# A hybrid decoder layer in fp32 on one core: the scheduler lays out the engines' streams by its timeline estimate instead of its plain one

## The chip, the cores and the metric

The kernel runs on one core of one Trainium2 chip. A core has TensorE (PE: matmuls, with its weight loads shown as PEld), VectorE (DVE), ScalarE (ACT), GpSimd (POOL) and SyncE (SP), each with an instruction stream of its own that it works off in order, and 16 DMA engines. The metric is device time in microseconds for one execution of the whole program; lower is better.

## The reference, cut to what matters

One layer, batch 1, 512 tokens, width 2048, everything in fp32. The layer's input is normalised and multiplied with one wide weight. Half of the mixing is done by 8 gated-DeltaNet heads, half by 8 latent-attention (MLA) heads. Then come an output projection with a residual, and a SwiGLU feed-forward network (FFN) of width 5632.

```
# gated DeltaNet, per head, in chunks (the kernel uses chunks of 128)
a_mat = where(strict, (k*beta) @ k.T * decay, 0)
sol   = triangular_solve(a_mat + I, [v*beta, k*beta*exp(gc)])
for each chunk:                       # one after the other
    v_new = u_c - w_c @ state
    o     = (q_c*exp(gc_c)) @ state + intra_c @ v_new
    state = state*exp(g_last) + k_dec.T @ v_new
# MLA, per head: softmax of (q_nope.k_nope + q_rope.k_rope), causal, times v
# FFN: (silu(h @ w_gate) * (h @ w_up)) @ w_down
```

## The kernel before, in words

The result has to be close to fp32, so each fp32 weight tile `raw` is split into a high part `whi` (cast on ACT, L137) and a rest `wlo` (subtraction on DVE, L138); activations are split likewise (`hh`, `hl`). A product of two split tiles is three matmuls into the same PSUM tile (`mm3`, L144 to L146). Weights are loaded by SP's queue; `raw` has two buffers, `whi` and `wlo` three each.

The program comes in four stages: the transposes and the norm of the input; the DeltaNet stage, which is what the change and the prediction speak of most; the MLA heads with the output projection; the FFN.

In the DeltaNet stage PE has two kinds of work. One is projections, `project(hp)` for head pairs 0 to 3, each with parts q, k, v and z, and then two `latent` projections for MLA. Each part takes two PSUM tiles `acc` (there are four), runs 96 mm3 matmuls into them and hands them to DVE: `u` (L440) is the read that frees an `acc` of parts q, k and v, and from it `y` is built (L441, L444 three times) and goes through ACT into `kq` or `vt`. `u` and `y` have one buffer each, `kq` two per head of a pair.

The other is `delta(h)`, one per head. Its first part squares and transposes k, multiplies `kq` with itself (the kk matmuls), makes `bm` (L500), `Y` (L513) and `dd` (L516, a reduction to the 16x16 diagonal blocks), sends `dd` to DRAM and back in another layout (`dr`, `rep`, two DMAs issued by ACT), and inverts the diagonal blocks by 30 short dependent DVE operations (`xt` L524 and `xs` L526), which give `R` (L527). Its second part, the chain, doubles the blocks in three levels (transposes of `R` at L555, two groups of small matmuls at L149, with DVE and ACT between them), and then goes through four chunks (`vn`, `st`). At its end ACT sums squares (L606), POOL takes a root (L169), DVE scales (`es`, L612), PE transposes (L617), and DVE writes `mixg` (L618). All of these matmuls use the PSUM tag `bank`, four tiles.

`project` and `latent` (the generator `fill`) and the two `delta` of a pair are generators; the strings ORDER and LAST say in which order their pieces are written into the program:

```
ORDER = "0ppp0p1ppp01p1"
LAST = "0ppp0p1ppp01ppp1"
```

What order the instructions then have on each engine is not written in the kernel: the tile scheduler of the context opened at L998 takes the program, its dependences and its buffers, and lays out one stream per engine, by priorities from the program's order and by an estimate of when each instruction could run. Names such as `acc_3005` below are a tile with the number of its allocation: `whi_3007`, `whi_3037`, `whi_3067` and `whi_3097` are the four weight tiles of pair 2's part z, whose PSUM tiles are `acc_3004` and `acc_3005`; `acc_2487` and `acc_2488` are those of its part k; head 2 has `R_1923`, head 3 `dd_2418` and `xt_2422`, head 6 `R_3943` and head 7 `R_4416`.

## Time and profile before

| | |
|---|---|
| median of 3 runs | 2429.13 us (2429.03 to 2430.13) |
| the profiled execution's own time | 2431.77 us |
| its span | 2430.0 us, mean granted TensorE clock 0.995 |
| PE busy | 2377.5 us (98%), 11142 matmuls |
| DVE busy | 1137.5 us (47%) |
| ACT busy | 706.8 us (29%) |
| POOL busy | 84.6 us (3%) |
| DMA | 225.74 MB, mean 93 GB/s |

The span is the time from the first to the last instruction on the core; the execution's own time has 1.77 us more around it. A row of a window table gives the busy time of each engine in that stretch, and how many of its instructions ran there. "PEclk" is the granted TensorE clock as a share of its full 2.4 GHz.

### The profile page before, as it was taken

To read this page: it belongs to the slowest core of one execution; us is meant where nothing else is said; L and a number is where in the kernel's file an instruction comes from. 1 tells how busy PE (TensorE), PEld (TensorE's weight loads), DVE (VectorE), ACT (ScalarE), POOL (GpSimd) and SP (SyncE) were. 2 spreads that over 40 slices of the span, in tenths; PEclk is the share of its full clock that TensorE was granted. 3 is DMA by queue.
4 is the path that set the end of the run, shared out by engine and by line. 5 is a ranking of instruction groups with operands and counts; after the bars stand their busy time and mean duration, and the time that the engine had idled before them with its cause. 6 is when DMAs were issued, how large, how long until landed. Compare 5 with 4: busy or idle time off the path is not lost.

```text
span 2430.0 us, 27609 instructions
## 1 busy us (share of the span) xinstructions
PE 2377.5 (98%) x11142; PEld 1954.5 (80%) x11142; DVE 1137.5 (47%) x1850; ACT 706.8 (29%) x1155; POOL 84.6 (3%) x89
## 2 busy tenths in 40 slices
PE   8999999999999999999999999999999999999998
PEld 6777878787787778888888888888888888888886
DVE  6556565655556555433434343433333343434345
ACT  5333333332333334322222212222222222222223
POOL 0010101110000000000000000000000000000000
PEclk9999999999999999999999999999999999999999
DMA  5322322222422222333333333232333333333333
GB/s 168 89 62 70 88 70 80 78 80 78 143 61 67 73 65 87 104 96 100 99 95 96 96 95 101 90 104 87 104 93 103 98 96 95 95 97 95 104 96 112
DMA packets 199807, 225.74 MB, mean 93 GB/s; under 512 B 17280, under 2 KB 161920, under 8 KB 199552
## 3 DMA queue, kind: packets, MB, share of 16 engines
q1 hardware_dynamic: 194752, 214.02, 29.4%
q10 hardware_dynamic: 4928, 9.97, 1.3%
q8 instruction: 87, 1.43, 0.3%
q14 instruction: 40, 0.33, 0.0%
HBM read 219.50 MB, written 4.46 MB: 92 GB/s over the span
## 4 chain that ended last, share of the span: by engine, by line
PE 87%; DVE 6%; DMA 3%; ACT 2%; issue 1%; POOL 1%; ACTq 0%; SPq 0%; POOLq 0%; DVEq 0%
PE acc L145 20%; PE acc L146 20%; PE acc L144 20%; PE bank L145 6%; PE bank L146 6%; PE bank L144 6%; PE bank L149 4%; DVE wlo L138 1%; PE score L149 1%; DMA rep<-dr 1%; DMA raw<-in_w_down 1%; PE op L149 1%; DVE y L444 1%; DMA raw<-in_w_in 1%; ACT whi L137 0%
## 5 line engine op out<-in xcount | busy, mean ns | idle before, releaser
L138 DVE TENSOR_TENSOR wlo<-raw,whi 128x1024 fp32r<-128x1024 f32 x386 | 469.0, 1216 | 705.7 <-ACT whi L137 701.0
L137 ACT CAST whi<-raw 128x1024 fp32r<-128x1024 f32 x386 | 403.6, 1046 | 1195.2 <-PE acc L145 650.0
L145 PE MATMUL acc<-fl,whi 128*128 128x512 f32 x1408 | 548.3, 389 | 0.0
L146 PE MATMUL acc<-fh,wlo 128*128 128x512 f32 x1408 | 548.2, 389 | 0.0
L144 PE MATMUL acc<-fh,whi 128*128 128x512 f32 x1408 | 548.1, 389 | 0.0
L145 PEld LDWEIGHTS acc<-fl,whi 128*128 128x128 f32 x1408 | 264.4, 188 | 54.8
L146 PEld LDWEIGHTS acc<-fh,wlo 128*128 128x128 f32 x1408 | 264.4, 188 | 54.8
L144 PEld LDWEIGHTS acc<-fh,whi 128*128 128x128 f32 x1408 | 264.3, 188 | 54.5
L145 PE MATMUL acc<-hl,whi 128*128 128x512 f32 (+1 forms) x656 | 264.4, 403 | 0.0
L144 PE MATMUL acc<-hh,whi 128*128 128x512 f32 (+1 forms) x656 | 262.1, 400 | 1.8 <-ACT whi L137 1.8
L146 PE MATMUL acc<-hh,wlo 128*128 128x512 f32 (+1 forms) x656 | 263.6, 402 | 0.0
L146 PE MATMUL bank<-whi,al 128*128 128x512 f32 x640 | 249.2, 389 | 0.0
L145 PE MATMUL bank<-wlo,ah 128*128 128x512 f32 x640 | 249.2, 389 | 0.0
L144 PE MATMUL bank<-whi,ah 128*128 128x512 f32 x640 | 249.2, 389 | 0.0
L924 DVE SCALAR_TENSOR_TENSOR x<-bank,rstd,x 128x512 f32<-128x512 f32 x160 | 119.8, 750 | 151.6 <-PE bank L146 151.6
L144 PEld LDWEIGHTS acc<-hh,whi 128*128 128x128 f32 (+1 forms) x656 | 124.3, 190 | 25.7 <-ACT whi L137 2.2
L145 PEld LDWEIGHTS acc<-hl,whi 128*128 128x128 f32 (+1 forms) x656 | 124.3, 190 | 24.5
L146 PEld LDWEIGHTS acc<-hh,wlo 128*128 128x128 f32 (+1 forms) x656 | 123.9, 189 | 23.5
L144 PEld LDWEIGHTS bank<-whi,ah 128*128 128x128 f32 x640 | 120.2, 188 | 24.9
L145 PEld LDWEIGHTS bank<-wlo,ah 128*128 128x128 f32 x640 | 120.2, 188 | 24.9
L146 PEld LDWEIGHTS bank<-whi,al 128*128 128x128 f32 x640 | 120.2, 188 | 24.9
L144 PE MATMUL acc<-whi,mgh 128*128 128x512 f32 x256 | 102.3, 400 | 2.8 <-ACT mgh L283 2.3
(284 smaller groups left out, 2228.1 us busy)
## 6 DMA issues: line engine op xcount, KB each, us to landing
raw<-in_w_gate SPq DMA_DIRECT2D x88, 512.0 KB, 3.6
raw<-in_w_up SPq DMA_DIRECT2D x88, 512.0 KB, 3.6
raw<-in_w_down SPq DMA_DIRECT2D x88, 512.0 KB, 3.8
raw<-in_w_in SPq DMA_DIRECT2D x80, 512.0 KB, 3.8
raw<-in_w_out SPq DMA_DIRECT2D x32, 512.0 KB, 4.0
rep<-dr ACTq DMA_DIRECT2D x8, 512.0 KB
x<-in_x ACTq DMA_DIRECT2D x4, 1024.0 KB, 7.8
raw<-in_w_ukv SPq DMA_DIRECT2D x32, 128.0 KB, 2.5
```

Of the source, the lines that this page charges most:

```text
L137: nc.scalar.copy(hi[:, :k * n], raw[:, :k * n])
L138: nc.vector.tensor_tensor(out=lo[:, :k * n], in0=raw[:, :k * n], in1=hi[:, :k * n].bitcast(F32), op=ALU.subtract)
L144: nc.tensor.matmul(ps, lhsT=lh, rhs=rh, start=start, stop=False)
L145: nc.tensor.matmul(ps, lhsT=lh, rhs=rl, start=False, stop=False)
L146: nc.tensor.matmul(ps, lhsT=ll, rhs=rh, start=False, stop=stop)
L149: nc.tensor.matmul(ps, lhsT=l, rhs=r, start=start, stop=stop)
L444: nc.vector.scalar_tensor_tensor(out=y, in0=u[:, j:j + S], scalar=vec[:, 0, j * 24 + ct:j * 24 + ct + 1], in1=y, op0=ALU.mult, op1=ALU.add)
L924: nc.vector.scalar_tensor_tensor(out=x2[:, t4, cs], in0=a, scalar=rstd[:, t4:t4 + 1], in1=x2[:, t4, cs], op0=ALU.mult, op1=ALU.add)
```

## The change

One argument of the tile context. The kernel's functions, buffers and operations stay as they are.

```diff
--- before.py
+++ after.py
@@ -995,7 +995,7 @@
     args.append(nc.dram_tensor("out_0", (S, D), F32, kind="ExternalOutput").ap())
-    with tile.TileContext(nc) as tc:
+    with tile.TileContext(nc, schedule_with_timeline_sim=True) as tc:
         layer_kernel(tc, *args)
```

The matmuls, the DVE operations and the DMA issues are the same in number; ACT has six more loads of a function table (L490 and the like), 18 for 12. What moves is the order on each engine. Three places follow.

The first is PE at the start of head 2's chain. Before, pieces of pair 2's part q (`acc_2124`) stand between its steps:

```order
L555 MATMUL bank_2186<-fst_68,R_1923 128x128 x4
L149 MATMUL bank_2187<-R_1923,bm_1904 128x64 x4
L144 MATMUL acc_2124<-hh_80,whi_2297 128x512
L145 MATMUL acc_2124<-hl_81,whi_2297 128x512
L146 MATMUL acc_2124<-hh_80,wlo_2298 128x512
...
L149 MATMUL bank_2198<-Y_1924,T_1922 128x64 x4
L146 MATMUL acc_2124<-hh_80,wlo_2298 128x512
L144 MATMUL acc_2124<-hh_80,whi_2297 128x512
L145 MATMUL acc_2124<-hl_81,whi_2297 128x512
L555 MATMUL bank_2204<-fst_68,R_1923 128x128 x4
```

After the change, the same steps:

```order
L146 MATMUL acc_3004<-hh_80,wlo_3068 128x512
L555 MATMUL bank_2186<-fst_68,R_1923 128x128 x4
L149 MATMUL bank_2187<-R_1923,bm_1904 128x64 x4
L149 MATMUL bank_2198<-Y_1924,T_1922 128x64 x4
L555 MATMUL bank_2204<-fst_68,R_1923 128x128 x4
L149 MATMUL bank_2205<-R_1923,bm_1904 128x64 x4
L149 MATMUL bank_2216<-Y_1924,T_1922 128x64 x4
L555 MATMUL bank_2222<-fst_68,R_1923 64x64 x4
```

and the end of that chain, up to the next projection matmul (`vn_2279` is the chain's last chunk, `kq_1113` belongs to head 3):

```order
L149 MATMUL bank_2247<-vn_2279,es_1903 128x128
L149 MATMUL bank_2403<-kq_1113 128x256 x2
L149 MATMUL bank_2409<-kq_1113 128x256 x2
L471 MATMUL bank_2470<-fst_68,vt_1873 128x128 x4
L471 MATMUL bank_2476<-fst_68,kq_1113 128x128 x4
L617 MATMUL bank_2689<-fst_68,es_1903 128x128 x4
L144 MATMUL acc_3005<-hh_80,whi_3007 128x512
```

The projections have moved ahead of the chain: when it begins, PE has done parts q, k and v of pair 2 and three of the four weight tiles of part z's first PSUM tile, and the 34 rows from L555 to L617 hold no projection matmul.

The second place is DVE around head 3's `dd`. Before, weight rests and the substitution follow it, and the read of pair 2's part k (`u_2618`) stands late in the substitution:

```order
L516 TENSOR_REDUCE dd_2418<-Y_2417 128x64
L138 TENSOR_TENSOR wlo_2581<-raw_2579,whi_2580 128x1024
L607 TENSOR_SCALAR ssq_2381<-ssq_2381 128x4
L138 TENSOR_TENSOR wlo_2631<-raw_2629,whi_2630 128x1024
L524 TENSOR_TENSOR xt_2422<-rep_2420,xs_2421 128x60
...
L524 TENSOR_TENSOR xt_2422<-rep_2420,xs_2421 128x16
L440 TENSOR_TENSOR u_2618<-acc_2488,rbc_71 128x512
```

After the change:

```order
L516 TENSOR_REDUCE dd_2418<-Y_2417 128x64
L441 TENSOR_SCALAR y_2610<-u_2609,vec_70 128x512
L618 SCALAR_TENSOR_TENSOR mixg_292<-bank_2689,vec_70,zt_2116 128x512
L444 SCALAR_TENSOR_TENSOR y_2610<-u_2609,vec_70,y_2610 128x512
L607 TENSOR_SCALAR ssq_2381<-ssq_2381 128x4
L444 SCALAR_TENSOR_TENSOR y_2610<-u_2609,vec_70,y_2610 128x512 x2
L440 TENSOR_TENSOR u_2618<-acc_2488,rbc_71 128x512
L441 TENSOR_SCALAR y_2619<-u_2618,vec_70 128x512
L524 TENSOR_TENSOR xt_2422<-rep_2420,xs_2421 128x60
...
L524 TENSOR_TENSOR xt_2422<-rep_2420,xs_2421 128x44
L138 TENSOR_TENSOR wlo_3098<-raw_3096,whi_3097 128x1024
```

The read that frees the PSUM tile of part k now stands right behind head 2's whole end and head 3's `dd`, and the rest of part z's last weight tile stands behind five of the `xt`.

The third place is PE at the end of the stage, heads 6 and 7. Before, pieces of the second latent projection (`acc_4896`, `acc_4897`) and of the output projection stand around head 7's last step:

```order
L146 MATMUL acc_4897<-hh_80,wlo_4900 128x512
L144 MATMUL acc_4896<-hh_80,whi_4929 128x512
...
L617 MATMUL bank_5018<-fst_68,es_4396 128x128 x4
L144 MATMUL acc_5130<-whi_5119,mgh_5055 128x512
```

After the change the last matmul of the latent projections stands ahead of head 6's chain:

```order
L146 MATMUL acc_4897<-hh_80,wlo_4990 128x512
L555 MATMUL bank_4204<-fst_68,R_3943 128x128 x4
...
L617 MATMUL bank_4720<-fst_68,es_3923 128x128 x4
L149 MATMUL bank_4636<-dg_4635,cst_67 128x128 x3
L555 MATMUL bank_4726<-fst_68,R_4416 128x128 x4
...
L617 MATMUL bank_5018<-fst_68,es_4396 128x128 x4
L149 MATMUL bank_5077<-cst_67,ssl_5066 128x128 x4
L144 MATMUL acc_5130<-whi_5119,mgh_5055 128x512
```

Both chains, 66 rows, stand between it and the next mm3 matmul, that of the output projection.

## Rows read from the trace of the kernel before

**Rows 1.** Windows by stage: each engine's busy time, then clock, DMA share, GB/s.

```profile
core 0: us, PE busy (x) PEld busy (x) DVE busy (x) ACT busy (x) POOL busy (x), PEclk, DMA share, GB/s
0.00:101.70 101.70, 90.03 (x410) 73.10 (x411) 61.81 (x95) 44.93 (x76) 2.58 (x13) 1.00 0.47 138
101.70:635.40 533.70, 511.84 (x2677) 417.30 (x2676) 319.14 (x758) 189.41 (x414) 60.66 (x58) 0.98 0.28 76
635.40:929.00 293.60, 286.40 (x1456) 231.03 (x1457) 173.85 (x347) 99.38 (x220) 18.16 (x13) 1.00 0.27 81
929.00:2350.00 1421.00, 1421.00 (x6306) 1178.04 (x6306) 536.34 (x583) 344.82 (x396) 1.01 (x1) 1.00 0.32 97
2350.00:2430.00 80.00, 68.26 (x297) 55.05 (x295) 46.39 (x68) 28.30 (x51) 2.18 (x4) 0.96 0.35 112
```

**Rows 2.** Windows around two long waits of PE and a short one.

```profile
143.00:147.20 4.20, 0.48 (x3) 0.09 (x2) 3.89 (x13) 1.05 (x1) 0.11 (x1) 0.96 0.47 135
147.20:153.00 5.80, 5.80 (x20) 5.12 (x21) 1.39 (x2) 0.59 (x1) 1.06 (x1) 0.50 0.38 114
570.00:576.00 6.00, 1.28 (x6) 0.77 (x6) 5.51 (x12) 2.19 (x3) 0.00 (x0) 0.80 0.31 87
576.00:582.00 6.00, 5.98 (x25) 4.88 (x26) 2.00 (x8) 0.00 (x0) 1.01 (x1) 0.63 0.32 87
630.00:636.00 6.00, 3.71 (x19) 2.71 (x17) 3.14 (x4) 2.85 (x5) 0.00 (x0) 1.00 0.55 149
```

**Rows 3.** PE in order of time: head 2's chain, then head 3's kk matmuls.

```profile
272.67 0.60 PE L555 MATMUL bank<-fst,R 128*128 128x128 f32 x4
...
277.45 0.60 PE L555 MATMUL bank<-fst,R 128*128 128x128 f32 x4
...
281.25 0.41 PE L555 MATMUL bank<-fst,R 64*64 64x64 f32 x4
...
292.71 0.48 PE L149 MATMUL bank<-vn,es 128*128 128x128 f32 x2
...
297.74 1.13 PE L149 MATMUL bank<-kq 128*128 128x256 f32 x4 [0.32 <-DVE es L612]
```

**Rows 4.** DVE in order of time, behind head 2's chain.

```profile
294.83 0.17 DVE L608 SCALAR_TENSOR_TENSOR sso<-sso,ssq 128x4 f32<-128x4 f32 x1
...
296.56 1.12 DVE L612 TENSOR_SCALAR es<-bank,f 128x128 f32<-128x128 f32 x4 [0.90 <-POOL f L169]
297.61 0.68 DVE L440 TENSOR_TENSOR u<-acc,rbc 128x512 f32<-128x512 f32 x1
...
299.26 1.22 DVE L138 TENSOR_TENSOR wlo<-raw,whi 128x1024 fp32r<-128x1024 f32 x1
...
307.53 1.04 DVE L516 TENSOR_REDUCE dd<-Y 128x64 f32<-128x512 f32 x1
...
319.37 0.26 DVE L524 TENSOR_TENSOR xt<-rep,xs 128x60 f32<-128x60 f32 x1 [5.67 <-DMA rep<-dr]
```

**Rows 5.** DVE in order of time: head 2's substitution, up to `R`.

```profile
257.65 0.26 DVE L524 TENSOR_TENSOR xt<-rep,xs 128x60 f32<-128x60 f32 x1 [4.46 <-DMA rep<-dr]
...
266.66 1.07 DVE L527 TENSOR_TENSOR R<-xs,cst 128x512 f32<-128x512 f32 x1
```

**Rows 6.** Groups by line, DVE: count, busy us, mean ns.

```profile
L444 DVE SCALAR_TENSOR_TENSOR y<-u,vec,y 128x512 f32<-128x512 f32 x72 | 54.0, 750 | 1.6
...
L440 DVE TENSOR_TENSOR u<-acc,rbc 128x512 f32<-128x512 f32 x24 | 16.5, 688 | 2.8 <-PE acc L146 1.9
L441 DVE TENSOR_SCALAR y<-u,vec 128x512 f32<-128x512 f32 x24 | 11.6, 482 | 0.6 <-ACT kq L452 0.5
...
L618 DVE SCALAR_TENSOR_TENSOR mixg<-bank,vec,zt 128x512 f32<-128x512 f32 x8 | 6.0, 745 | 2.1 <-PE bank L617 2.1
```

**Rows 7.** Waits of PE by line and releaser: us in total, times, longest.

```profile
PE bank L555 <- DVE R L527: 6.0, 4, 3.7
...
PE score L149 <- ACT knh L283: 2.7, 4, 0.7
...
PE bank L145 <- DVE fl L138: 1.7, 2, 1.1
```

## The prediction

> **What bounds the kernel now.** I read the windows by stage first. From 929 to 2350 us, the FFN and the end of the output projection, PE is busy for all of the 1421 us, 6306 matmuls at 0.2253 us each [rows 1]. No order of the same matmuls can shorten that stretch; it can only stay or get longer. What an order can change lies in the DeltaNet stage (101.7 to 635.4), where PE is busy 511.84 of 533.70 us and so idle 21.9, in the MLA stage with 7.2 idle, and in the end with 11.7 [rows 1]. The clock of the DeltaNet stage is 0.98, so some 10 us of it went to half speed (0.02 of 511.84). Some 32 us are thus all that a better order could find there.
>
> The timeline of PE shows why the loss is that small. Head 2's chain takes 20.0 us from its first L555 to its last `vn` row [rows 3], and 39 projection matmuls stand in it; at 0.2253 they take 8.8 of it, so the chain's own matmuls take 11.2. The chain is a ladder of short matmuls with DVE and ACT operations between them, and the projections fill its waits. The table of waits agrees: all waits for an `R` that is late come to 6.0 us in 4 places [rows 7].
>
> The last view is DVE behind a chain. From the last `vn` at 292.71 to the end of the next head's `dd` (307.53 + 1.04 = 308.57) it takes 15.9 us, and `rep` lets the first `xt` start only 10.8 later, at 319.37 [rows 3, 4]. From there to the end of `R` it is 10.1 us (257.65 to 267.73) [rows 5]. An `R` is thus 31.7 us late on the kk matmuls (from 297.74: 10.8 + 10.8 + 10.1). That is the longest ladder of the kernel, and PE passes it unharmed only if it has projections enough that need nothing from DVE.
>
> **The change, part by part.** No operation is added but six ACT table loads, and ACT is busy 189 of 533.7 us in that stage [rows 1], so I cost them at nothing; the slack of ACT hides them. Everything else is place. In the new order PE runs the projections ahead, and later has chains with nothing in them. Where it waits, it waits in order, and all behind it waits too.
>
> a. *The joints.* Behind head 2's chain PE's next projection matmul is the first into `acc_3005`. All four `acc` tiles are taken, so it needs the read `u_2618`, and DVE's order puts that behind head 2's end and all of head 3's first part. From the last `vn` to the end of `dd` it is 15.9 us as measured [rows 3, 4]. In those 15.9, from 296.56 on, DVE also did one L440, one L441, three L444 and a `wlo`, which in the new order are elsewhere: 0.69 + 0.48 + 3 x 0.75 + 1.22 = 4.6 [rows 4, 6]. If DVE was the limit, the new path is 11.3, if the latencies of ACT and POOL were (DVE waited 0.90 for POOL here), it is 15.9. Behind `dd` come L441, L618, three L444, a short `ssq` and L440: 0.48 + 0.75 + 2.25 + 0.17 + 0.69 = 4.3 (the short one as `sso`) [rows 4, 6]. Sum 15.6 to 20.2. PE has two pairs of kk and three groups of transposes of its own then, some 3.3 (2 x 1.13 less their overlap, 3 x 0.4 to 0.6) [rows 3]. PE stands 12.3 to 16.9; I take 14. The order repeats this at three joints, behind heads 0, 2 and 4: **42 us**.
>
> b. *The weight behind it.* After the joint PE has 36 projection matmuls and two more before it needs `wlo_3098`: 38 x 0.2253 = 8.6 us. On DVE that subtraction stands behind five `xt`. The first can start 10.8 after `dd`, which is 6.5 after `u_2618`; then come four `xs`, the other `xt`, six L444, L440, L441 and the `wlo` itself: 9 x 0.24 + 6 x 0.75 + 0.69 + 0.48 + 1.22 = 9.0 [rows 4, 5, 6]. So 15.5 against 8.6, a wait of 6.9, three times: **21 us**. It falls to nothing only if `rep` lands earlier.
>
> c. *Chains without filling.* Head 2's levels took 4.78 and 3.80 [rows 3]; the first had a `wlo` of 1.22 in DVE's way. I take an empty chain at 18.1, some 2 less than the 20.0 with its filling, and 11.2 of it is PE's own work: 6.9 idle. Heads 2 and 4 stand like that, half of head 0's, and a part of the odd heads' (2.7, and 2 x 2): 2 x 6.9 + 6.7 = **20 us**. The lower end is 15, the upper 24.
>
> d. *`R` of the even heads.* Between head 2's kk matmuls and its L555 PE has 96 projection matmuls and some small ones, 24 us; `R` comes 31.7 behind the kk, or less where DVE has less in between. Wait 0 to 8, I take 6 for heads 2 and 4 each. Head 6 has only 60, 16 us: wait 10 to 16, I take 14. Together **26 us**.
>
> e. *The end.* Behind the last latent matmul head 6's chain stands empty (6.9), then head 7's first part, whose `R` comes after 11.3 to 15.9, and 10.8, and 8.5 to 10.1 (with fewer foreign rows): 30.6 to 36.8, less 5 us of small matmuls, so 28; then head 7's chain (6.9) and its end up to L617, of which the path from `vn` to `es` is 5.0 (292.71 to 297.68) [rows 3, 4]. Before, latent matmuls stood in all of these. **47 us**.
>
> f. *The clock.* After an idle of 3.7 us PE ran 5.8 us at a granted 0.50, the lower level of 1.2 GHz; after one of 4.7, six at 0.63 [rows 2]. That is 2.9 us lost for each long wait. The joints and the wait of head 7 are four: **12 us**.
>
> g. *What is won.* In the MLA stage the matmuls that waited for `knh`, 0.7 at a time [rows 7], and for `v` have other work ahead of them now: some 1.4 for each of four pairs, 5.6 us. At the end eight matmuls move into a wait for `fl`, at most 1.1 + 0.7 [rows 7]: 1.8. Together **-7**. In the FFN the order changes too, but PE had no wait there and DVE and ACT keep their order: nothing, unless a weight comes late.
>
> Sum of the losses: 42 + 21 + 20 + 26 + 47 + 12 = 168. The old waits of the stage are replaced, not kept, since a to f count the new ones from zero: of the 32 us, the wait at 143 and the slow clock behind it (3.7 + 2.9) stay, so 26 go. 168 - 26 - 7 = +135. The profiled execution took 2431.8; its median is 2429.1, 2.6 below. **2431.8 + 135 - 2.6 = 2564 us.** With the lower ends (a 37, b 15, c 15, d 10, e 43, f 0, and all 32 replaced) it is +81; with the upper (51, 23, 24, 32, 52, 20) +169.
>
> **The rivals.** *R1, faster.* The steps that are spread find the 26 us that I only replace, and the 7, and the new waits don't arise because the projections that run ahead read and free `acc` early: 2429.1 - 33 = 2396. It decides at the joints: as soon as a to f come to less than 33 together. For it speaks that heads 1, 3 and 5 have their first levels spread over 21 to 26 projection matmuls a step, which is better than before; against it that the end alone (e) has no projection left to fill with. Chance 0.05.
>
> *R2, the joints are hidden.* `u_2618` is not late, since DVE reaches it while PE is still in the chain, so a, b and three of four f fall: 168 - 42 - 21 - 9 = 96, and 96 - 33 = +63: 2489. For it: DVE is busy only 60% of the stage [rows 1]. Against: `dd` stands ahead of it and needs the chain's end. Chance 0.16.
>
> *R3, the clock stays low.* In the short matmuls of an empty chain PE is idle a third of the time. If it never gets back to full clock there, the 11.2 us of a chain's own matmuls take up to 11.2 more in each of some five chains, 56, in place of f: +179, 2608. For it: the window of 570 to 576, PE busy 1.28 of 6, had 0.80 granted and the next 0.63 [rows 2]. Against: 630 to 636 had 2.3 us idle and stayed at 1.00 [rows 2]. Chance 0.11. The Trainium skill, page "TensorE: Matmul & The Clock Gate", section "HAM oscillation — how this bites in real kernels", speaks for this rival: a PE that falls idle between bursts is throttled again and begins each burst cold; by that rule all empty chains would be slow, while the row of 630 to 636 shows a short idle that cost no clock, so that the trace agrees for the long waits only.
>
> *R4, no difference.* The moved rows all lie in waits that PE had anyway. Chance 0.02; the 34 rows of head 2's chain without a projection matmul speak against it.
>
> My forecast, 0.66, and these four make 1. **2564 us, range 2480 to 2615**, from R2 to a little above R3. What differs by under 0.2% (5 us) can't be told from no change here. Faster 0.05, same 0.03 (R4, and a near miss of R1), slower 0.92.
>
> **What would show it.** The FFN's stretch must stay at full PE: 1421 us for the same matmuls. The whole gain or loss must lie ahead of the MLA stage. PE must wait for `u` (L440) at an `acc` matmul three times, 12 to 17 us each, then for a `wlo` three times for 7; for `R` at L555 some 26 us more than before, and once for about 28 near the end. The granted clock must fall to 0.5 or so behind each of these and be back 6 us later. I am wrong if waits for `u` are missing (R2), if the clock lies low through the chains (R3), if a wait for weights shows in the FFN, or if `dd` comes so early that a is below 10.

## The result and the profile after

The changed kernel takes 2559.8 us (median of 4 runs, 2557.4 to 2563.8), the kernel before 2429.6 (4 runs): a ratio of 1.053, 95% interval 1.052 to 1.055. The forecast was 2564. The profiled execution took 2560.4 us; its span is 2558.6, 128.6 more than before.

Windows of the changed kernel by stage, cut at 101.7 as before and then where the next stages begin (columns as in [rows 1]):

```profile
101.70:775.40 673.70, 555.13 (x2664) 456.03 (x2663) 319.32 (x758) 196.44 (x420) 47.90 (x58) 0.87 0.23 67
...
1068.00:2489.00 1421.00, 1421.00 (x6307) 1177.61 (x6306) 537.37 (x583) 345.38 (x397) 1.01 (x1) 1.00 0.32 97
```

The DeltaNet stage is 673.7 us long for 533.7, and the FFN's stretch is what it was, 1421 us for 6307 matmuls (6306 in [rows 1]). In the stage PE is idle 118.6 us (673.70 - 555.13) for 21.9, and busy 555.1 for 511.8 with 13 matmuls fewer (21 of the stage's projection matmuls stand before 101.7 in the changed kernel, and some small ones come in at the end), at a mean granted clock of 0.87 for 0.98. So 97 of the 140 us are waits, and 43 are matmuls at the lower clock. From the stage's end to the first FFN matmul it is 334.0 us for 342.3, and from there to the end of the span 1449.1 for 1452.2: 8.3 and 3.1 won. 140.0 - 8.3 - 3.1 = 128.6.

The table of PE's waits of the changed kernel (as [rows 7]):

```profile
PE bank L555 <- DVE R L527: 35.1, 4, 18.2
PE acc L144 <- DVE u L440: 23.9, 5, 5.9
PE bank L471 <- DVE es L612: 10.0, 4, 2.7
PE bank L149 <- ACT qe L490: 9.7, 4, 2.4
...
PE acc L146 <- DVE wlo L138: 2.8, 5, 1.2
```

The waits for `u` that the order announced are there, at 5.9 us each in the joints, not the 12 to 17 that the prediction named as a sign. Ahead of each stand smaller ones, which the timeline of PE shows at the joint behind head 2's chain:

```profile
370.19 0.49 PE L149 MATMUL bank<-vn,es 128*128 128x128 f32 x2
...
373.96 1.13 PE L149 MATMUL bank<-kq 128*128 128x256 f32 x4 [2.42 <-ACT qe L490]
377.83 1.12 PE L471 MATMUL bank<-fst,vt 128*128 128x128 f32 x4 [2.74 <-DVE es L612]
380.06 1.12 PE L471 MATMUL bank<-fst,kq 128*128 128x128 f32 x4 [1.11 <-DVE vb L543]
...
387.95 0.79 PE L144 MATMUL acc<-hh,whi 128*128 128x512 f32 x1 [5.93 <-DVE u L440]
388.55 0.63 PE L145 MATMUL acc<-hl,whi 128*128 128x512 f32 x1
...
392.38 0.41 PE L145 MATMUL acc<-hl,whi 128*128 128x512 f32 x1
```

From the last `vn` to the projection it is 17.8 us (370.19 to 387.95). The idle is in four pieces, 12.2 together, since the second pair of kk and two groups of transposes wait for pieces of the same ladder. Behind the joint a projection matmul takes 0.63 and begins 0.43 after the one ahead; from 392.38 on it is 0.4 and 0.23. DVE at the same place:

```profile
381.79 1.00 DVE L516 TENSOR_REDUCE dd<-Y 128x64 f32<-128x512 f32 x1
...
387.21 0.69 DVE L440 TENSOR_TENSOR u<-acc,rbc 128x512 f32<-128x512 f32 x1
...
391.89 0.25 DVE L524 TENSOR_TENSOR xt<-rep,xs 128x60 f32<-128x60 f32 x1 [3.39 <-DMA rep<-dr]
...
398.24 1.21 DVE L138 TENSOR_TENSOR wlo<-raw,whi 128x1024 fp32r<-128x1024 f32 x1
```

`dd` ends 12.6 us behind the last `vn` (15.9 in [rows 3, 4]); `rep` is there 9.1 us later (10.8 in [rows 4]). Windows over head 2's chain, head 4's, and head 7's, each from its first L555 on:

```profile
346.20:370.20 24.00, 19.25 (x106) 16.99 (x106) 4.67 (x13) 2.12 (x4) 0.20 (x1) 0.64 0.00 0
505.00:530.40 25.40, 20.67 (x106) 18.35 (x106) 4.68 (x13) 2.12 (x4) 0.18 (x1) 0.60 0.00 1
...
743.80:770.00 26.20, 20.66 (x102) 18.13 (x102) 4.67 (x13) 2.49 (x6) 0.00 (x0) 0.61 0.00 1
```

An empty chain takes 24 to 25 us at a mean granted clock of 0.60 to 0.64, and in heads 2 and 4 4.7 of it are idle. With its filling it took 20.0 [rows 3]. The mean is made of two levels. Seven stretches of the stage, of 17 us or more, lie at the lower one throughout; four of them, and the sum of the seven:

```profile
348.00:365.10 17.10, 13.57 (x66) 12.28 (x67) 2.85 (x8) 1.54 (x3) 0.00 (x0) 0.50 0.00 0
375.30:392.40 17.10, 7.53 (x23) 5.77 (x24) 11.20 (x30) 5.98 (x22) 3.78 (x5) 0.50 0.13 33
505.00:525.50 20.50, 16.65 (x80) 15.20 (x81) 3.11 (x8) 2.12 (x4) 0.18 (x1) 0.50 0.00 1
...
713.20:764.40 51.20, 23.52 (x108) 21.11 (x109) 25.31 (x79) 10.49 (x30) 4.65 (x4) 0.50 0.04 11
sum 167.40, PE 93.57 PEld 81.15 DVE 74.19 ACT 37.67 POOL 17.57; mean PE 13.37 PEld 11.59 DVE 10.60 ACT 5.38 POOL 2.51
```

Of PE's 93.6 us in them, 23.4 are in the three joints and 70.2 in the chains of heads 2, 4, 6 and 7 with what stands between the last two. At full clock the same matmuls would take about half (an estimate), so the clock cost PE some 12 us in the joints and 35 in the chains.

### The profile page after: what moved, and what is told of

Its sections match the earlier page's. It is cut to its first block, busy times and chain, and to the rows that moved or that the text cites. A ratio compares the mean times of both kernels' runs of the same rounds, so it can differ in the third digit from the quotient of the medians.

```text
span 2558.6 us, 27586 instructions
## 1 busy us (share of the span) xinstructions
PE 2418.9 (95%) x11142; PEld 1996.6 (78%) x11142; DVE 1141.2 (45%) x1850; ACT 713.1 (28%) x1161; POOL 71.4 (3%) x89
## 4 chain that ended last, share of the span: by engine, by line
PE 88%; DVE 5%; ACT 3%; DMA 3%; issue 1%; ACTq 0%; SPq 0%; POOL 0%; POOLq 0%; DVEq 0%
PE acc L144 21%; PE acc L146 20%; PE acc L145 20%; PE bank L144 6%; PE bank L145 6%; PE bank L146 6%; PE bank L149 4%; DMA rep<-dr 2%; PE score L149 1%; PE op L149 1%; DMA raw<-in_w_down 1%; PE bank L555 1%; DVE xt L524 1%; DVE y L444 1%; DVE xs L526 0%
## 5 line engine op out<-in xcount | busy, mean ns | idle before, releaser
L144 PE MATMUL acc<-hh,whi 128*128 128x512 f32 (+1 forms) x656 | 262.1, 400 | 26.0 <-DVE u L440 23.9
L144 PE MATMUL bank<-whi,ah 128*128 128x512 f32 x640 | 239.2, 389 | 0.0
## 6 DMA issues: line engine op xcount, KB each, us to landing
x<-in_x ACTq DMA_DIRECT2D x4, 1024.0 KB, 12.2
```

The source lines that it names most:

```text
L144: nc.tensor.matmul(ps, lhsT=lh, rhs=rh, start=start, stop=False)
```

## The experiments

All run on the kernel before or on the changed one with one edit. The ratios are against the kernel before, run beside each.

**Where the loss is: one part at a time.** A part of the program can be put into a block that is laid out for itself. Three kernels: all behind the DeltaNet stage in such a block, laid out as before (`rest_plain`) or by the timeline estimate (`rest_tl`), and everything up to the end of the DeltaNet stage in a block by the timeline estimate, the rest as before (`gdn_tl`). The edit of the first two:

```diff
+    with tc.block(schedule_with_timeline_sim=True):   # rest_tl; False in rest_plain
     banks(op=1, score=3, acc=2, bank=2)
...
```

> The kernel before, with everything behind the DeltaNet stage put into a block of its own that is still laid out by the plain estimate: the control for the two kernels that change the layout of one part only. If a block boundary costs little: 2429 to 2434 us. If it costs a restart of every engine: 2440 or more.

> The DeltaNet stage by the plain estimate, all behind it by the timeline estimate. Theory 1 (the parts add up: the changed kernel won 8.2 us between the start of the output projection and the first FFN matmul and 3.1 us behind that, and lost 140 in the DeltaNet stage): 8 to 11 us less than the control with a plain block, some 2420 us, faster than both kernels. Rival (what the changed kernel won there came only from weights that were loaded while its DeltaNet stage stood still): within 2 us of the control.

> The DeltaNet stage by the timeline estimate, in the same order as in the changed kernel, all behind it by the plain one. Theory 1: the whole loss is there, and the 11 us that the changed kernel won behind it are missing: 2566 to 2575 us. Rival (part of the loss arises later, from weights that come in another order): under 2555.

`rest_plain` took 2437.1 us (1.002, 1.001 to 1.003), `rest_tl` 2428.5 (0.999, 0.998 to 1.000), `gdn_tl` 2570.8 (1.058, 1.056 to 1.059). Windows from the first output-projection matmul to the first FFN matmul, of `rest_plain` and then of `rest_tl`:

```profile
639.60:986.20 346.60, 339.22 (x1695) 275.30 (x1696) 202.37 (x380) 123.60 (x265) 18.01 (x13) 0.99 0.26 79
```

```profile
637.00:976.90 339.90, 333.87 (x1697) 274.91 (x1697) 204.69 (x380) 123.75 (x267) 18.01 (x13) 0.99 0.27 80
```

The parts add up: the loss is in the DeltaNet stage alone, and the timeline order wins 8.6 us in the rest. The block boundary of `rest_plain` costs about as much (6.6 us, between its two expectations), so that `rest_tl` ends 2 us under the kernel before, with an interval that touches no change. In `gdn_tl` no such cost shows: 2570.8 is the changed kernel's 2559.8 and 11.0, close to the 11.4 won behind the stage. `rest_tl` is the fastest version found; I don't call it faster.

**The waits for `u`: two buffers for `y`.**

```diff
-                y = gd.tile([P, S], F32, name="y", tag="y", bufs=1)
+                y = gd.tile([P, S], F32, name="y", tag="y", bufs=2)
...
```

> The changed kernel with two buffers for y instead of one, so that DVE can read a projection out of PSUM before the result ahead of it has gone into kq. The scheduler then puts 25 projection matmuls into the chains of heads 2 and 4 (0 before). Theory 1 (the joints are waits for acc tiles that DVE frees late): the waits of PE for u, 23.9 us, nearly vanish, and with 25 x 0.225 us of filling in two chains it is 20 to 35 us less than the changed kernel, 2525 to 2540. Rival 2 (the waits only move to the next thing that is late, R or the kk matmuls): within 5 us of 2560. Rival 3 (what costs is the low clock behind any wait): half of theory 1.

2558.3 us (1.052, 1.051 to 1.054): no gain. The table of waits of this kernel:

```profile
PE bank L555 <- DVE R L527: 31.4, 2, 18.6
PE acc L144 <- DVE u L440: 21.3, 2, 10.8
PE acc L144 <- DVE zt L432: 10.9, 3, 3.6
```

Where five waits for `u` stood there are two of up to 10.8, and three for `zt`. The waits moved, as rival 2 says; theory 1 falls for this buffer.

**The end: projections held back for heads 6 and 7.** A kk matmul and the third chunk of each chain are remembered, and the first matmul of a latent's PSUM tile gets an ordering dependence on them.

```diff
+    PINS = {(CQ0, 1): ("kk", 6), (CKV0, 0): 6, (CKV0, 1): ("kk", 7)}
...
+        if behind in mark:
+            tc.add_manual_dep(m.ins, mark[behind], mybir.DependencyInfo(
+                mybir.DependencyClass.NoSync, mybir.DependencyReason.DATA), reason="behind")
```

> The changed kernel with three of the last projections held back: the second half of the first latent behind head 6's kk matmuls, the halves of the second latent behind head 6's chain and head 7's kk matmuls. Between kk and R of head 6 PE then has 96 projection matmuls instead of 60, of head 7 139 instead of none, head 5's chain has 71 instead of 291. Theory 1 (the end is idle because nothing is left to fill it): the wait for head 7's R (18.2 us) and the one ahead of it (2.4) vanish, that for head 6's R (11.8) falls to about 5, and the clock holds: 30 to 45 us less, 2515 to 2530. Rival 1 (the end is as long as its own ladder of DVE, DMA and ACT, and the projections only move): within 8 us of 2560. Rival 2 (it is the clock): 10 to 15 less.

2527.5 us (1.040, 1.039 to 1.042): 32 us less, theory 1. The waits for `R` and `u` in this kernel:

```profile
PE acc L147 <- DVE u L446: 20.8, 4, 5.9
...
PE bank L562 <- DVE R L534: 5.5, 2, 3.1
```

The two long waits for `R` are gone (35.1 to 5.5), the joints stay.

**The end alone, in the plain order.**

```diff
-LAST = "0ppp0p1ppp01ppp1"
+LAST = "0pppppppppp01011"
```

> The kernel before, plain estimate, with the order string of the last head pair changed so that all the latent projections are written ahead of head 6's chain: 475 projection matmuls stand between head 6's kk matmuls and its R (139 before), none in head 6's chain, none behind. It does the end of the changed kernel alone. Theory 1: what the end cost there, 46 us of idle and some 10 to 15 of low clock, less what the old end waited (about 8): 2470 to 2490 us. Rival (the end only looks idle, its ladder has this length anyway): under 2445.

2477.2 us (1.020, 1.018 to 1.021): +47 us, as expected of the end with its low clock. Its DeltaNet stage has 53.1 us idle for 21.9, and 527.0 busy for 511.8, so some 31 of the 47 are waits and 15 the clock:

```profile
101.70:681.80 580.10, 527.02 (x2681) 431.16 (x2681) 322.68 (x763) 190.87 (x417) 59.43 (x58) 0.94 0.28 78
```

PE's longest wait is again that for head 7's `R`:

```profile
PE bank L555 <- DVE R L527: 23.9, 5, 18.1
```

**The low clock: matmuls that nobody reads.** First into the tile that DVE reads next (`warm`), then into another (`warm2`).

```diff
+        def warm(tile, n):
+            for _ in range(n if h in (2, 4, 6, 7) else 0):
+                nc.tensor.matmul(tile[:, HALF * NT:2 * HALF * NT], lhsT=hh[:, 0, 0:P], rhs=hh[:, 1, 0:HALF * NT],
+                                 start=True, stop=True)
...
+            warm(dp, 3)      # warm2: behind the operation that reads zp
...
+            warm(zp, 3)      # behind the one that reads dp
...
+            warm(sp, 2)      # behind the copy to vn
```

> The changed kernel with 120 matmuls added that nobody reads (three of 128x256 behind each step of the chains of heads 2, 4, 6 and 7, into unused columns of the same PSUM tiles), to keep the clock up there; the outputs are unchanged. PE was busy 555 us in the DeltaNet stage instead of 512 with the same matmuls: 43 us are a lower clock. Rival 2 (the low clock is on the path in the chains): the granted clock in these chains rises to near 1.00 and it is 10 to 25 us less, 2535 to 2550. Theory 1 (the chains are bound by DVE and ACT between the matmuls, and the clock costs little there): within 5 us of 2560, up to 8 more for the added matmuls.

> The added matmuls that nobody reads once more, but placed so that no DVE operation waits for them: behind the operation that reads the step's result is written, into PSUM columns of another tile (three of 128x256 per wait in the levels, two in the chunks, heads 2, 4, 6 and 7). If they get the granted clock of the empty chains up from 0.60 to near 1.00, a chain falls from 24 to some 18 us: 20 to 28 us less than the changed kernel. If the clock stays low in spite of them: 0 to 10 more, and the price of the low clock is left to the rows.

`warm` took 2588.4 us (1.065, 1.063 to 1.066), which neither theory had. PE at the start of head 2's chain:

```profile
348.06 1.00 PE L149 MATMUL bank<-R,bm 128*128 128x64 f32 x8
348.87 0.60 PE L459 MATMUL bank<-hh 128*128 128x256 f32 x3
350.08 1.94 PE L149 MATMUL bank<-Y,T 128*128 128x64 f32 x8 [0.61 <-DVE Y L571]
```

DVE waits for the added matmuls too, since they write the tile that it reads, and then takes its 0.61 as before. So the 120 matmuls went onto the path: from the first L555 to the last `vn` the four chains take 29.6, 29.8, 31.2 and 31.6 us for 23.9, 25.4, 25.3 and 25.2, together 22 of the 28.6 us lost. This run tells nothing about the clock, but that a matmul that the next DVE operation has to wait for costs its time.

`warm2` took 2560.6 us (1.054, 1.052 to 1.055), no different from the changed kernel. Windows over its chains of heads 2, 4 and 6:

```profile
346.70:371.00 24.30, 19.67 (x141) 16.24 (x141) 5.53 (x15) 6.74 (x19) 1.62 (x3) 1.00 0.00 1
```

```profile
499.90:525.00 25.10, 23.79 (x130) 21.34 (x131) 4.73 (x14) 2.12 (x4) 0.20 (x1) 0.66 0.00 1
676.00:702.00 26.00, 24.73 (x129) 22.29 (x129) 4.68 (x13) 2.12 (x4) 0.24 (x1) 0.63 0.00 1
```

In head 2's chain the clock held, and its last `vn` came 19.2 us behind its first L555 (346.65 to 365.83) for 23.9: that is the price of the clock in one chain, 4.7 us, and the step from head 2's `R` to head 3's fell from 63.4 to 58.5. (The first window goes 5 us beyond that `vn`.) In the others, head 7's too, the clock was low in spite of the added matmuls, and the whole won nothing. Why it held in one only is open.

**The buffers of `kq`.**

```diff
-        heads[hp] = [{"kq": gd.tile([P, 2, S], F32, name="kq", tag="kq")} for _ in range(2)]
+        heads[hp] = [{"kq": gd.tile([P, 2, S], F32, name="kq", tag="kq", bufs=4)} for _ in range(2)]
...
-        lat = gd.tile([P, NT, S], F32, name="lat", tag="lat", bufs=1)
+        lat = [gd.tile([P, 2, S], F32, name="lat", tag="kq", bufs=4) for _ in range(2)]
```

> The changed kernel with four buffers of kq instead of two (the latents' tile takes two of them, so that the pool still fits). A pair's q and k need then not wait in DVE's queue until the pair before has used its own. In the order that the scheduler makes of it the chains of heads 1 to 5 have 91, 105, 92, 200 and 52 projection matmuls (172, 0, 172, 0, 291 before); heads 6 and 7 stay empty. Theory 1 (the joints and the empty chains of heads 2 and 4 come from kq's two buffers): their waits (13.4 us at each of three joints, 3.2 twice for u, 7 and 6 of low clock in each of two chains) vanish, the end stays: 50 to 75 us less, 2485 to 2510. Rival (as with two buffers for y, the wait moves to the next buffer): within 10 us of 2560.

> As the run with four kq buffers, and the second half of the first latent and the halves of the second held back behind the kk matmuls of heads 5, 6 and 7: 96 projection matmuls between kk and R of each, none in their chains. Theory 1: the R waits of heads 6 and 7 (11.8 and 18.2) become 6 each, head 5's new one is 6 too, and its chain is now empty (7 idle and 6 of low clock more): 0 to 20 us less than the run with four kq buffers alone, still 40 or more above the kernel before, since three chains stand empty. Rival (nothing but the joints and the wait for head 7's R mattered): within 10 us of the kernel before.

2548.7 us (1.049, 1.048 to 1.050) and, with the projections of the end held back, 2522.4 (1.039, 1.037 to 1.040). The first is a miss: 11 us won for 50 to 75 expected. Its waits:

```profile
PE bank L555 <- DVE R L527: 47.9, 6, 19.5
...
PE acc L144 <- DVE zt L432: 6.7, 2, 4.3
```

No wait for `u` is left (23.9 before this edit), but those for `R` went from 35.1 to 47.9 and `zt` took 6.7. So the joints are not what costs by itself. The second run is 26 us under the first, a little more than its 0 to 20.

**What is conserved.** These misses led to another reading: from one head's `R` to the next a ladder has to be climbed (chain, end, `bm`, `dd`, two DMAs, 30 operations of DVE), and PE's projections lie beside it. The table gives the time from the first L555 of a head's chain to that of the next, from the timelines of PE, and in brackets the number of projection matmuls that the order puts between them.

| us (matmuls) | head 0 to 1 | 1 to 2 | 2 to 3 | 3 to 4 | 4 to 5 | 5 to 6 | 6 to 7 |
|---|---|---|---|---|---|---|---|
| before | 64.6 (192) | 60.9 (192) | 62.1 (192) | 60.8 (192) | 61.9 (192) | 60.8 (192) | 70.1 (192) |
| changed | 87.3 (232) | 95.1 (300) | 63.4 (84) | 95.4 (300) | 65.3 (85) | 112.4 (359) | 61.2 (0) |
| `y2` | 104.3 (324) | 96.1 (279) | 61.6 (108) | 95.2 (276) | 61.7 (105) | 96.7 (268) | 62.1 (0) |
| `kq4` | 103.7 (340) | 86.3 (243) | 69.6 (141) | 88.9 (244) | 92.3 (280) | 68.7 (112) | 61.9 (0) |
| `kq4pin` | 103.4 (340) | 85.7 (243) | 68.3 (141) | 87.6 (244) | 71.8 (200) | 60.0 (96) | 66.7 (96) |
| `pin` | 87.2 (232) | 95.5 (300) | 63.4 (84) | 95.4 (300) | 65.0 (85) | 67.7 (167) | 78.4 (185) |
| `last_early` | 64.0 (192) | 60.8 (192) | 62.2 (192) | 60.8 (192) | 61.8 (192) | 140.3 (528) | 53.8 (0) |
| `even` | 73.3 (182) | 73.3 (202) | 71.9 (182) | 74.7 (202) | 72.2 (182) | 72.3 (202) | 67.3 (158) |

In the timeline orders a step takes some 62 us with no projection at all, and hardly more with 85 or 105. Above that it grows by about 0.24 us for each matmul (72 at 190, 112 at 359: 40 us for 169), close to PE's own pitch of 0.2253 [rows 1], with strays of some 6 us. The 62 are no fixed length: in the plain order of `last_early` an empty step takes 53.8. The kernel before has 192 everywhere and 61: there PE's work and the ladder just cover each other. In the changed kernel a step with 300 pays 34 more, and the one with 84 beside it gives nothing back. The last run tests this.

```diff
+    PINS = {(CQ0, 0): ("kk", 6), (CQ0, 1): 6, (CKV0, 0): ("kk", 7), (CKV0, 1): 7}
+    for i in range(3):
+        PINS.update({(i + 1, 0): ("kk", 2 * i), (i + 1, 1): 2 * i, (i + 1, 2): ("kk", 2 * i + 1),
+                     (i + 1, 3): 2 * i + 1})
```

> The changed kernel, timeline estimate, with the first matmul of each projection part held back: q and v of the next pair behind the kk matmuls of the even and the odd head, k and z behind the third chunk of their chains, the latents likewise with heads 6 and 7. From one head's R to the next PE then has 182 to 202 projection matmuls (232, 268, 84, 268, 85, 351 and 0 in the changed kernel). New theory (a head's ladder takes 60 us however little PE has to do beside it, so that what counts is how evenly the projections lie on the heads; a wait that is taken away at one buffer only comes back at another): 62 to 75 us from R to R, 2440 to 2495. Rival (the joints' buffers or the empty chains' low clock cost by themselves, and the order of the scheduler for the rest): the levels of the chains are still empty, so no better than the best run so far, 2520 or more.

(The counts of the changed kernel in it leave out the matmuls between a chain's end and the next kk; the table has them.) 2497.2 us (1.028, 1.026 to 1.030), 2 above the expected range in all, the steps inside theirs (67 to 75), and far under the rival's 2520. No wait for `u` is left in its table. The run gives back 63 of the 130 us, and the window of its DeltaNet stage shows which:

```profile
101.70:712.60 610.90, 550.67 (x2679) 461.82 (x2678) 317.86 (x758) 191.93 (x416) 49.67 (x58) 0.90 0.25 70
```

PE is idle 60.2 us there for 118.6 in the changed kernel, but busy 550.7 for 555.1. So evenness took away half of the waits and little of the low clock. What remains over the kernel before, 77 us of the stage, is half idle (60.2 for 21.9) and half clock (550.7 for 511.8): the levels of the chains still have no filling. No run fills them with projections in this order, so that this last step is read from rows and not tested. PE at the first level of head 2:

```profile
295.70 0.66 PE L566 MATMUL bank<-fst,R 128*128 128x128 f32 x4 [2.16 <-DVE R L538]
296.19 1.06 PE L158 MATMUL bank<-R,bm 128*128 128x64 f32 x8
300.74 1.94 PE L158 MATMUL bank<-Y,T 128*128 128x64 f32 x8 [3.49 <-DVE Y L576]
```

**The MLA waits, by hand.** One dependence in the plain order, the first score matmul of a pair behind its v projection.

```diff
+                if j == 0 and i == 0 and h % 2 == 0:
+                    tc.add_manual_dep(m.ins, vlast[0], mybir.DependencyInfo(
+                        mybir.DependencyClass.NoSync, mybir.DependencyReason.DATA), reason="behind")
```

> The kernel before, plain estimate, with one addition: the first score matmul of each MLA head pair is held behind the first half of the pair's v projection, as the timeline order has it in spirit. Theory (the waits for knh, 2.7 us, and knl, 1.7, are what the timeline order won there): 2 to 4 us less than the kernel before, 2426 to 2428. Rival (what it won lies at the start of the stage and in weight order): within 1 us.

2431.1 us (1.0005, 0.9996 to 1.0013), no difference. The waits for `knh` (2.7 us) are gone from its table, those for `knl` grew from 1.7, and one for `t` is new:

```profile
PE acc L144 <- DVE knl L284: 2.9, 4, 0.7
...
PE acc L144 <- DVE t L295: 1.9, 4, 0.5
```

So the waits moved here too, and nothing was won. Of the timeline order's 8.3 us up to the first FFN matmul, 4.0 are less idle (7.1 to 3.1); where the rest comes from is open.

## Why the prediction was right, step by step

The direction, the place and the sum were right, 2564 for 2560. That the sum came within 4 us is in good part luck, for its terms are less good:

| term | predicted us | measured us | from |
|---|---|---|---|
| a, joints | 42 | 35 | idle between the last `vn` and the projection: 11.2, 12.2, 12.0 |
| b, weight behind it | 21 | 2.8 | the waits for `wlo` |
| c, empty chains | 20 | 14.5 | idle in the chains of heads 2 and 4: 4.75 and 4.73; in those of heads 0, 1 and 3: 0.88, 2.07 and 2.07 |
| d, `R` of even heads | 26 | 17 | 35.1 less head 7's 18.2 |
| e, the end | 47 | 40 | idle from 670.5 to 775.4, 51.3, less 11.7 for head 6's `R`, which is in d |
| f, clock | 12 | 43 | busy 555.1 for 511.8, so net of what the kernel before lost |
| not foreseen | 0 | 6 | two waits for `u` of some 3 us in part z |
| g, won behind the stage | -7 | -11 | 8.3 and 3.1 |

Sorted by kind, the prediction had some 138 us more idle (a to e, less the old waits) and some 4 more at low clock (f, less the old); the stage has 97 and 43. The two errors, 41 too many and 39 too few, cancel. Of the old waits it kept 6.6 us for that ahead of head 0's `R`; in the changed kernel that wait is gone.

*a and e* had the right mechanism: both follow paths that the trace of before had row by row, and the paths were the same. a, with 35, lies just under its lower end of 37. `pin` and `last_early` confirm that the end costs, by taking it away (32 us) and by putting it in alone (47, of which 31 are waits); the size of e is that of the waits alone.

*b* is the step that failed. It took `rep` at 10.8 us behind `dd`, counted DVE's operations end to end, 9.0, and gave PE full clock. At head 2's joint `rep` came after 9.1, `u` ended 5.1 behind `dd` and not 4.3, the operations took 7.6 from the first `xt` to the end of the `wlo` (391.89 to 399.45), and PE ran its first ten matmuls at half clock, so that it needed 11.4 us for what was put at 8.6. Four errors of 0.8 to 2.8 us ate a wait of 6.9. A term that is the difference of two long paths is as uncertain as both.

*d* was 9 us too high: head 6 waited 11.7 for 14, heads 2 and 4 2.1 and 3.1 for 6 each. But these two waits have a cause that the prediction put at nothing, the six more table loads, with the reason that ACT has slack. (The traces hold 25 loads for 19, not 18 for 12.) In heads 2 and 4 two of them stand with the work on `zt` between `qe` and `es`, which follow one another at once in the kernel before (242.08 and 242.57), and DVE's `bm` needs `es`. ACT and DVE behind head 2's kk matmuls:

```profile
316.60 0.60 ACT L490 ACTIVATE qe<-bank 128x512 f32<-128x512 f32 x1
317.21 1.28 ACT L433 ACT_TABLE_LOAD   x1
318.51 0.63 ACT L433 ACTIVATE zt<-zt 128x512 f32<-128x512 f32 x1
319.16 1.28 ACT L488 ACT_TABLE_LOAD   x1
320.45 0.63 ACT L488 ACTIVATE es<-es 128x512 f32<-128x512 f32 x1
...
321.12 1.12 DVE L500 SCALAR_TENSOR_TENSOR bm<-bank,s,es 128x128 f32<-128x128 f32 x4 [4.75 <-ACT es L488]
```

DVE waits for `es` 14.1 us in 4 places, for 0.9 in one before. The loads and `zt` make 3.2 us of the path from kk to `R` (1.28 + 0.63 + 1.28), more than either of PE's two waits; that PE would not have waited without them is an estimate, and no run takes them away. A share of busy time over a stage says nothing of an operation that stands between two links of a ladder.

*f* was mis-sized by 31 us, and its mechanism was too narrow. It charged the low clock only to the 6 us behind each long wait [rows 2], 9 for the joints and 3 for the wait for head 7's `R`. In the joints it was some 12. But the clock also stood at the lower level for 17.1 us of head 2's empty chain and 20.5 of head 4's, and in the end for 51.2 without a break: some 35 us by the same estimate. A clock that lies low through the chains was one of the prediction's own signs of being wrong, and it came true. Rival R3 had the mechanism right for these chains, at a price of 56. The row that I set against it, 630 to 636 with 2.3 us of idle and a clock of 1.00 [rows 2], was one wait; the chains have one after the other. That c came out lower may be the other side of this: a chain at 0.64 has less idle and takes longer.

*That waits add up* was an assumption of the whole sum, and the runs refute it as a price list. Without the waits for `u` (`kq4`) the changed kernel gains 11 us, not 24 and more, as the ladder's length comes out at the next place; along one order the waits do follow one another, and there they may be summed. Part of what was lost is the evenness: 192 projection matmuls beside each head's ladder became 300 and 84, and `even` wins 63 us by undoing that. The rest, the clock above all, it leaves.

*R2* (its own sum, 2429 + 63, gives 2492 and not 2489) is refuted by the waits for `u` in the joints; *R1* by the DeltaNet stage, 140 us longer; *R4* by the result. On the low clock, the Trainium skill's section "HAM oscillation — how this bites in real kernels" (page "TensorE: Matmul & The Clock Gate") says that a PE that idles between bursts begins each of them cold; its example has a wait of some microseconds before each burst. The trace agrees for the joints, where ten matmuls at 0.43 follow waits of 12.2 us in 17.8. The chains (0.60 to 0.64 granted, with idles of 0.5 to 0.6 us between the steps) are not its case, so that the prediction read it too widely when it had all empty chains slow by that rule, though they were slow. Nor does the section say why in `warm2`, with most of these idles filled, one chain ran at 1.00 and three stayed at 0.63 to 0.66.

## What to carry to other kernels

Where a ladder of short dependent operations runs beside a long row of independent matmuls, count how many of these the order puts beside each rung before costing single waits: what is above PE's share on one rung was lost here, and what was missing on another wasn't won back. An order that runs independent work ahead as soon as it is ready looks busy at first and pays at the end, where nothing is left to fill with (some 32 us here). A saving or a cost on an engine with slack is judged by where it stands in the ladder, not by the engine's share. A buffer that is added at the place of a wait should be judged by the time, not by that wait: here it came back at another place twice, and a third time with a dependence (`vpin`).

## What the runs showed of the hardware

- The granted clock stayed low with PE busy for most of the time: 0.64 with 19.25 of 24.00 us busy in head 2's chain. With added matmuls it was 0.66 at 23.79 of 25.10 in head 4's chain, and 1.00 at 19.67 of 24.30 in head 2's. What tells these apart is not settled. In one chain that kept full clock the time fell from 23.9 to 19.2 us.
- At half clock a projection matmul began 0.43 us after the one ahead, for 0.23.
- A table load of ACT took 1.28 us each time, and two of them with 0.63 us of work between them stood ahead of an operation that DVE waited 4.75 us for (head 2, at 321.12).
- A block boundary in the program cost 6.6 us in `rest_plain` (2437.1 for 2430.6); in `gdn_tl` none of it shows. In `rest_tl` PE's first matmul behind it waited 6.3 us for the cast of a weight:

```profile
637.03 1.22 PE L144 MATMUL acc<-whi,mgh 128*128 128x512 f32 x2 [6.30 <-ACT whi L137]
```
